# A decoder trunk's gMLP output projection: seven block products in place of eight

## The chip, the core and the metric

The kernel runs on one core of a Trainium2 chip. The metric is the time of one execution on the device in microseconds (us), from the first instruction to the last with the start and the end of the program around it. Lower is better. A run's profile is one execution taken by the hardware profiler; its span goes from the first to the last instruction.

The names in the text: TensorE (PE) multiplies matrices and writes to PSUM, which has eight buffers of 128 x 512 floats here; VectorE (DVE), ScalarE (ACT) and GpSimd (POOL) work element by element; SyncE (SP) issues most of the transfers (DMA) between the device's memory and the on-chip SBUF. Each engine works through its own queue in order.

## The reference

A trunk of two layers on 512 tokens of 1024 features. Layer 0 mixes tokens with a gMLP, then comes a gated feed-forward net with a short convolution, then a gated embedding; layer 1 has attention in place of the gMLP. The part that the change touches is the last line of the gMLP:

```python
def mixer_a(xn, w_in, g_v, w_s, b_s, w_out):
    z = jax.nn.gelu(xn @ w_in)
    u, v = jnp.split(z, 2, axis=-1)
    v = rmsnorm(v, g_v)
    ...
    s = jnp.einsum('hts,bcshd->bcthd', w, v) + b_s.T.astype(v.dtype)[None, None, :, :, None]
    s = s.reshape(B, S, A_WIDTH)
    return (u * s) @ w_out
```

Its result is added to the residual stream h, and the norm of the feed-forward net (norm_ffn) reads h next. All data are 32-bit floats.

## The kernel before, in words

Activations lie transposed, with features on the 128 partitions and the 512 tokens along the free axis: h is eight tiles h[0] to h[7] of 128 x 512. To keep float32 accuracy with TensorE's float32r, every operand x is split into a high part (a cast) and a low part (x minus the cast), and each product takes three matmuls: high by high, high by low, low by high (`mm3`, line 218; its matmul is line 229, so all stages' matmuls carry that line and are told apart by the tile they write).

Weights come in pieces of 1 MB from memory. The list of pieces, in the order in which the stages use them, is made ahead (lines 71 to 131). `load` (162) brings a piece into one of three staging buffers that take turns (tags r0 to r2, `staged`, 143). `pump` (173) cuts it into units of at most 128 x 1024 and splits each: the cast into `wh` is ACT's (line 197), the low part `wl` is DVE's (198). There are four buffers each for wh and wl, and a stage asks for units up to four ahead (`chunk`, 208), so a cast waits until matmuls have let go of an earlier unit.

A dense stage (`dense_add`, 423) runs over four chunks of 256 output features. A chunk has two units of weights; for each of its two output tiles, 8 x 3 matmuls of 512 columns add up in one PSUM buffer "d", then DVE adds it to h (431) and `Norm.take` (341) does three things with the new h tile: the split with the gain (ACT 302, DVE 303), the square (ACT 332), and the running sum of squares "acc" (POOL 337, for the last tile DVE). When all eight are in, DVE turns and reduces the sum (350, 352), TensorE adds it across partitions ("ms", 361), and the factor 1/rms goes out to memory and back to lie in rows ("line", "rstd", 376 and 401).

The feed-forward net has a second form of a stage already, the woven one (`woven_add`, 478). It takes activation tiles in pairs: tile 2p and 2p+1, each cut into a first and a second half of 256 tokens, are a 2 x 2 block matrix; the weights of 256 output features are another. Their product takes seven block products in place of eight (a scheme of Strassen's kind), over sums and differences of the blocks. `Pair` (445) makes the activations' seven operands: "edge" is the first half of tile 2p, "own" is tile 2p+1, "ones" and "twos" are differences. `begin` is called when the first tile of the pair is there, `end` when the second is. `weave` (149) makes the weights' sums on DVE (157 to 159) in a further staging buffer, "wsum", and a chunk has then three units of 1024 and one of 512. The seven products of 256 columns each add into two PSUM buffers: "dx" (a chain from which partial results "head" and "tail" are copied out by ACT) and "dy". DVE adds them to h (497, 513, 524, 525). A chunk's seventh product (number 4) is done late, inside the next chunk (`close`, 493).

The gMLP, with the names of the lines: values zv[0] to zv[3] (tiles m0 to m3) hold v; for each chunk c of 4, two tiles of u are projected (751), scaled (DVE 756), passed through GELU (ACT 758); TensorE forms "s" from zv and the masked position weights (761), DVE adds gain and bias (764) and multiplies (767), and the result is split into two tiles of the arena (770). Then `dense_add` at line 773 does the output projection. Every stage's TensorE work is issued in the order of the program as far as the data are expected in time; the compiler that orders each engine's queue may put an instruction that it expects to be ready ahead of one that it does not.

Two lines say how arena and m-tiles are used as homes for a pair's own, ones and twos:

```python
437	        if q < SLOTS:
438	            return [ap.tile([P, S], F32R, tag=f"a{x}{q}", name=f"{name}{x}") for x in "hl"]
439	        both = mp.tile([P, 2, S], F32R, tag=f"m{q - SLOTS}", name=name)
```

## Time and profile before

| what | before |
|---|---|
| median of 3 runs | 1121.63 us (1121.51 to 1121.77) |
| profiled execution | 1120.52 us |
| its span | 1118.8 us |
| mean granted TensorE clock | 0.998 |
| values and u chunks of the gMLP | to 98.5 us |
| output projection (tile d) | 100.28 to 143.81 us |
| feed-forward net's first woven stage | 242.07 to 283.25 us |

A row of a timeline has the start in us from the span's start, the time in us, the engine, the line, the operation and what it wrote from what; x2 at the end means two instructions merged, and the bracket says how long the engine had been idle and what released it. A row of the chain of work that ended last has start, time and what. A row of a tile's view has the line, engine, operation, count, and the duration in ns as least, median and greatest. Matmuls overlap, so the time of one (390 ns for 512 columns) is longer than the step from one to the next.

### The profile page before, as it was taken

To read this page: it belongs to the slowest core of one execution; us is meant where nothing else is said; L and a number is where in the kernel's file an instruction comes from. 1 tells how busy PE (TensorE), PEld (TensorE's weight loads), DVE (VectorE), ACT (ScalarE), POOL (GpSimd) and SP (SyncE) were. 2 spreads that over 40 slices of the span, in tenths; PEclk is the share of its full clock that TensorE was granted. 3 is DMA by queue.
4 is the path that set the end of the run, shared out by engine and by line. 5 is a ranking of instruction groups with operands and counts; after the bars stand their busy time and mean duration, and the time that the engine had idled before them with its cause. 6 is when DMAs were issued, how large, how long until landed. Compare 5 with 4: busy or idle time off the path is not lost.

```text
span 1118.8 us, 14875 instructions
## 1 busy us (share of the span) xinstructions
PE 1108.8 (99%) x5691; PEld 947.1 (85%) x5691; DVE 868.3 (78%) x1374; ACT 568.9 (51%) x936; POOL 103.9 (9%) x167
## 2 busy tenths in 40 slices
PE   9999999999999999999999999999999999999997
PEld 7888888889888998888888887888898889988876
DVE  5566449999788877657988997499997898785696
ACT  5733325545444544554656776255454445445543
POOL 1100210000000000022204451100000000000210
PEclk9999999999999999999999999999999999999999
DMA  8632313223331252333134224321244212522433
GB/s 296 135 114 76 113 48 113 76 76 123 142 113 39 76 189 69 101 113 113 63 88 132 76 57 151 111 93 71 76 151 136 90 38 76 189 85 88 148 103 86
DMA packets 35624, 118.40 MB, mean 106 GB/s; under 512 B 11800, under 2 KB 17440, under 8 KB 25056
## 3 DMA queue, kind: packets, MB, share of 16 engines
q1 hardware_dynamic: 34800, 116.19, 31.8%
q0 software_dynamic: 336, 0.79, 0.4%
q8 instruction: 45, 0.74, 0.3%
q10 hardware_dynamic: 416, 0.46, 0.1%
q14 instruction: 27, 0.22, 0.1%
HBM read 109.02 MB, written 2.11 MB: 99 GB/s over the span
## 4 chain that ended last, share of the span: by engine, by line
PE 68%; DVE 20%; ACT 4%; DMA 4%; issue 3%; POOL 0%; POOLq 0%; SPq 0%; ACTq 0%; DVEq 0%
PE up L229 26%; PE d L229 7%; PE dx L229 5%; DVE wl L198 5%; PE dy L229 4%; PE gate L229 4%; PE u L229 4%; PE q L229 3%; DVE c L558 3%; DVE c L559 2%; PE o L229 2%; DVE hs L551 2%; ACT wh L197 1%; PE v L241 1%; PE v L239 1%
## 5 line engine op out<-in xcount | busy, mean ns | idle before, releaser
L198 DVE TENSOR_TENSOR wl<-wraw,wh 128x1024 fp32r<-128x1024 f32 (+2 forms) x198 | 232.8, 1177 | 83.4 <-ACT wh L197 82.1
L197 ACT CAST wh<-wraw 128x1024 fp32r<-128x1024 f32 (+2 forms) x197 | 194.1, 990 | 147.9 <-PE up L229 56.1
L229 PE MATMUL up<-nf00h,wh 128*128 128x512 f32 x352 | 137.1, 390 | 0.0
L229 PE MATMUL up<-nf10h,wh 128*128 128x512 f32 x352 | 137.0, 389 | 0.0
L229 PE MATMUL up<-nf10l,wh 128*128 128x512 f32 x352 | 137.0, 389 | 0.0
L229 PE MATMUL up<-nf00l,wh 128*128 128x512 f32 x352 | 137.0, 389 | 0.0
L229 PE MATMUL up<-nf00h,wl 128*128 128x512 f32 x352 | 136.9, 389 | 0.0
L229 PE MATMUL up<-nf10h,wl 128*128 128x512 f32 x352 | 136.9, 389 | 0.0
L557 ACT ACTIVATE c<-hs,vec 128x512 f32<-128x512 f32 x88 | 71.6, 815 | 64.4 <-DVE hs L551 62.6
L558 DVE SCALAR_TENSOR_TENSOR c<-hs,vec,c 128x511 f32<-128x511 f32 x88 | 65.5, 747 | 20.4 <-ACT c L557 20.4
L229 PEld LDWEIGHTS up<-nf10h,wh 128*128 128x128 f32 x352 | 66.1, 188 | 13.7
L229 PEld LDWEIGHTS up<-nf00h,wl 128*128 128x128 f32 x352 | 66.1, 188 | 13.7
L229 PEld LDWEIGHTS up<-nf10l,wh 128*128 128x128 f32 x352 | 66.1, 188 | 13.7
L229 PEld LDWEIGHTS up<-nf00l,wh 128*128 128x128 f32 x352 | 66.1, 188 | 13.6
L229 PEld LDWEIGHTS up<-nf00h,wh 128*128 128x128 f32 x352 | 66.1, 188 | 13.6
L229 PEld LDWEIGHTS up<-nf10h,wl 128*128 128x128 f32 x352 | 66.1, 188 | 13.5
L559 DVE SCALAR_TENSOR_TENSOR c<-hs,vec,c 128x510 f32<-128x510 f32 x88 | 65.6, 748 | 2.2
L197 ACT CAST wh<-wsum 128x1024 fp32r<-128x1024 f32 x32 | 33.7, 1052 | 35.3 <-PE dy L229 11.3
L551 DVE TENSOR_TENSOR hs<-up,nf1rstd 128x512 f32<-128x512 f32 x44 | 30.1, 686 | 21.1 <-DMA nf1rstd<-nf1line 10.5
L551 DVE TENSOR_TENSOR hs<-up,nf0rstd 128x512 f32<-128x512 f32 x44 | 30.1, 686 | 20.9 <-DMA nf0rstd<-nf0line 10.4
L198 DVE TENSOR_TENSOR wl<-wsum,wh 128x1024 fp32r<-128x1024 f32 x32 | 39.1, 1221 | 9.3 <-ACT wh L197 9.2
L562 ACT ACTIVATE a<-c 128x512 f32<-128x512 f32 x44 | 27.7, 630 | 15.9 <-DVE c L559 15.8
(519 smaller groups left out, 2661.4 us busy)
## 6 DMA issues: line engine op xcount, KB each, us to landing
wraw<-in_w_up SPq DMA_DIRECT2D x44, 1024.0 KB, 4.8
wraw<-in_w_down SPq DMA_DIRECT2D x16, 1024.0 KB, 4.8
wraw<-in_w_gate SPq DMA_DIRECT2D x8, 1024.0 KB, 5.3
wraw<-in_w_down SPq DMA_DIRECT2D x8, 768.0 KB, 4.1
wraw<-in_w_u SPq DMA_DIRECT2D x4, 1024.0 KB, 10.8
wraw<-in_w_out SPq DMA_DIRECT2D x4, 1024.0 KB, 4.7
wraw<-in_w_q SPq DMA_DIRECT2D x4, 1024.0 KB, 4.8
wraw<-in_w_o SPq DMA_DIRECT2D x4, 1024.0 KB, 4.9
```

Of the source, the lines that this page charges most:

```text
L197: cast = nc.scalar.copy(hi, src)
L198: state["split"] = splits[u] = cast, nc.vector.tensor_sub(low, src, hi.bitcast(F32))
L229: nc.tensor.matmul(ps, w, x, start=first and j == 0, stop=last and j == len(todo) - 1, skip_group_check=onto)
L239: nc.tensor.matmul(ps, xh[:, s], wh[:, a:b], start=st, stop=False)
L241: nc.tensor.matmul(ps, xh[:, s], wl[:, a:b], start=False, stop=en)
L551: ins = nc.vector.tensor_mul(hs, ps, rstds[1])
L557: nc.scalar.activation(c, hs, AF.Identity, bias=v("conv_b", l * 2 * NJ + col), scale=cw[2])
L558: nc.vector.scalar_tensor_tensor(c[:, 1:], hs[:, : S - 1], cw[1], c[:, 1:], op0=ALU.mult, op1=ALU.add)
L559: nc.vector.scalar_tensor_tensor(c[:, 2:], hs[:, : S - 2], cw[0], c[:, 2:], op0=ALU.mult, op1=ALU.add)
L562: nc.scalar.activation(a, cs[0], AF.Silu)
```

## The change

The output projection of the gMLP calls `woven_add` instead of `dense_add`, and its weights are planned as woven pieces. The eight tiles u x s are made into four pairs as they come, with the arena's tiles 0 to 8 as homes for pairs 0 to 2 and m0 to m2 (the value projection's tiles) for pair 3. `Pair` is given its homes as an argument; with `soon`, which is set for pair 3, it makes the parts that the first products need first. `woven_add` learns to feed the norm, to use other buffers for head and tail (c0 and c1), and with `soon` to do product 5 ahead of product 2 in the first chunk. The feed-forward net's stages keep their behaviour. The diff, cut:

```diff
@@ -114,7 +114,7 @@
     for q, k0, k1 in FIRST:
         plan_pair(t["w_v"][2 * q : 2 * q + 2], k0, k1)
     plan_cols(t["w_u"], 4, KD)
-    plan_cols(t["w_out"], 4, KD)
+    plan_woven(t["w_out"], 4, 0, KD)
     plan_ffn(0)
     plan_cols(t["w_gate"][0], 4, KD)
     plan_cols(t["w_kv"][0:1], 1, KD)
@@ -445,26 +445,34 @@
     class Pair:
 
 
-        def __init__(self, p, edge, name):
-            self.p, self.name = p, name
+        def __init__(self, p, edge, name, homes):
+            self.homes, self.name = homes[3 * p : 3 * p + 3], name
             self.edge = edge[:, p, 0, :], edge[:, p, 1, :]
 
-        def begin(self, a):
+        def begin(self, a, soon=False):
             self.a = a
-            self.own, self.ones, self.twos = (couple(homes[3 * self.p + x], f"{self.name}_{x}") for x in range(3))
+            self.own, self.ones, self.twos = (couple(q, f"{self.name}_{x}") for x, q in enumerate(self.homes))
             hi, lo = self.edge
             nc.scalar.copy(hi, a[:, first])
             self.t = tp.tile([P, S], F32, tag="acc", name=f"{self.name}t")
             nc.vector.tensor_sub(self.t[:, first], a[:, first], a[:, second])
             nc.vector.tensor_sub(lo, a[:, first], hi.bitcast(F32))
-
-        def end(self, b):
+            if soon:
+                split(self.t[:, first], *(x[:, first] for x in self.ones))
+
+        def end(self, b, soon=False):
             t, u = self.t, tp.tile([P, S], F32, tag="sq", name=f"{self.name}u")
+            if soon:
+                split(b, *self.own)
             nc.vector.tensor_sub(t[:, second], b[:, second], self.a[:, second])
             nc.vector.scalar_tensor_tensor(u[:, first], t[:, first], -1.0, b[:, second],
                                            op0=ALU.mult, op1=ALU.subtract)
             nc.vector.scalar_tensor_tensor(u[:, second], u[:, first], -1.0, b[:, first],
                                            op0=ALU.mult, op1=ALU.subtract)
+            if soon:
+                split(u, *self.twos)
+                split(t[:, second], *(x[:, second] for x in self.ones))
+                return
             for src, (hi, lo) in ((b, self.own), (t, self.ones), (u, self.twos)):
                 split(src, hi, lo)
 
@@ -475,7 +483,7 @@
                           7: (self.ones, second), 6: (self.twos, first), 4: (self.twos, second)}[x]
             return [z[:, cols] for z in pair]
 
-    def woven_add(pairs, between):
+    def woven_add(pairs, between=None, norm=None, tags=("acc", "sq"), soon=False):
 
 
         ops = {x: [p.operand(x) for p in pairs] for x in range(1, 8)}
@@ -495,20 +503,28 @@
                 product(4, chain, w, 0, first=False)
                 nc.scalar.copy(tail[:, first], chain)
                 nc.vector.tensor_sub(h[2 * c + 1], h[2 * c + 1], tail)
+                if norm is not None:
+                    norm.take(2 * c + 1)
             return run
 
         late = None
         for c in range(4):
             top, low = h[2 * c], h[2 * c + 1]
             chain, other = psum(f"dx{c}")[:, first], psum(f"dy{c}")
-            head = tp.tile([P, S], F32, tag="acc", name=f"head{c}")
-            tail = tp.tile([P, S], F32, tag="sq", name=f"tail{c}")
+            head = tp.tile([P, S], F32, tag=tags[0], name=f"head{c}")
+            tail = tp.tile([P, S], F32, tag=tags[1], name=f"tail{c}")
             w = unit()
             product(1, chain, w, 0)
-            product(2, other[:, first], w, n)
-            nc.scalar.copy(head[:, first], chain)
-            w = unit()
-            product(5, other[:, second], w, n)
+            if c or not soon:
+                product(2, other[:, first], w, n)
+                nc.scalar.copy(head[:, first], chain)
+                w = unit()
+                product(5, other[:, second], w, n)
+            else:
+                nc.scalar.copy(head[:, first], chain)
+                w, w2 = unit(), w
+                product(5, other[:, second], w, n)
+                product(2, other[:, first], w2, n, first=False)
             product(6, chain, w, 0, first=False)
             nc.vector.tensor_sub(low[:, second], low[:, second], other[:, second])
             nc.scalar.copy(head[:, second], chain)
@@ -523,8 +539,10 @@
                     nc.scalar.copy(tail[:, second], chain)
             nc.vector.tensor_add(top, top, head)
             nc.vector.tensor_add(top, top, other)
+            if norm is not None:
+                norm.take(2 * c)
             late = close(c, chain, unit(), tail)
-            if c == 0:
+            if c == 0 and between:
                 between()
         late()
 
@@ -575,7 +593,7 @@
                 edge = at.tile([P, PAIRS, 2, N], F32R, tag="vtl", name=f"edge{i}")
                 pairs = []
                 for p in range((j1 - j0) // 2):
-                    pair = Pair(p, edge, f"act{i}_{p}")
+                    pair = Pair(p, edge, f"act{i}_{p}", homes)
                     pair.begin(up(j0 + 2 * p) if p else ahead)
                     pair.end(up(j0 + 2 * p + 1))
                     pairs.append(pair)
@@ -743,7 +761,8 @@
     for c in range(NC):
         nc.vector.tensor_scalar_mul(zv[c], zv[c], rv[:, c : c + 1])
 
-    us = []
+    edge = at.tile([P, PAIRS, 2, N], F32R, tag="vtl", name="edge")
+    us = [Pair(c, edge, f"us{c}", range(3 * PAIRS)) for c in range(PAIRS)]
     for c in range(4):
         parts = chunk(256, KD)
         ups = [psum(f"u{c}_{j}") for j in range(2)]
@@ -765,12 +784,9 @@
                 s.rearrange("p (b t) -> p b t", b=NC), sp.rearrange("p (b t) -> p b t", b=NC), v("a_norm_v", m),
                 bS[:, m : m + 1, :].to_broadcast([P, NC, P]), op0=ALU.mult, op1=ALU.add)
             nc.vector.tensor_mul(u, u, s)
-            hi = ap.tile([P, S], F32R, tag=f"ah{m}", name=f"ush{m}")
-            lo = ap.tile([P, S], F32R, tag=f"al{m}", name=f"usl{m}")
-            split(u, hi, lo)
-            us.append((hi, lo))
+            (us[c].end if j else us[c].begin)(u, soon=c == 3)
     nf = Norm("nf0", [(xp, "x", gain("norm_ffn", 0))])
-    dense_add(us, KD, nf)
+    woven_add(us, norm=nf, tags=("c0", "c1"), soon=True)
 
 
     lines = dram.tile([KD, 2, P], F32, name="lines")
```

## Prediction

> **What bounds the kernel now.** The page comes first: how full is TensorE?
>
> ```profile
> span 1118.8 us, 14875 instructions
> PE 1108.8 (99%) x5691; PEld 947.1 (85%) x5691; DVE 868.3 (78%) x1374; ACT 568.9 (51%) x936; POOL 103.9 (9%) x167
> ```
>
> TensorE (PE) is busy for all but 10 us. Time is won where it issues less work, or lost where it is made to wait. The profiled execution took 1120.52 us (1118.8 us of span and 1.72 us around it), 1.11 us less than the median of the three timed runs, 1121.63 us. I make the sum against the execution and carry its difference over to the median.
>
> Second, the chain of work that ended last, around the stage that is changed:
>
> ```profile
> 98.50 1.78 PE s L761 x16
> 100.28 43.53 PE d L229 x192
> 143.81 0.22 PE turned L781 x2
> 144.03 5.46 PE up L229 x24
> 149.49 0.13 PE nf0ms L361 x2
> ...
> 164.95 1.29 DVE hs L551 x2
> ```
>
> The output projection is the row "d": 192 matmuls of 512 columns in 43.53 us, 0.2267 us each, with no hole before, inside or behind it. The two things that follow are pinned to its end: the up projection, and the norm's small matmul nf0ms at 149.49, from which the broadcast of the norm's factor and all gating of the feed-forward net hang (VectorE's "hs" at 164.95; from there the chain runs mostly on VectorE). So what counts is by how much nf0ms moves.
>
> Third, the stretches: how much room have the other engines beside TensorE, and how much in the feed-forward net's stage that has the woven form already?
>
> ```profile
> 60.00:100.00 40.00, 40.00 (x210) 34.28 (x209) 25.20 (x33) 16.49 (x22) 0.00 (x0) 1.00 0.23 81
> 100.00:144.00 44.00, 44.00 (x198) 36.39 (x197) 22.95 (x29) 17.41 (x24) 9.33 (x6) 1.00 0.28 96
> 242.00:284.00 42.00, 41.86 (x342) 41.15 (x341) 37.21 (x50) 22.03 (x37) 0.00 (x0) 1.00 0.40 136
> ```
>
> The columns are the stretch, its length, then PE, PEld, DVE, ACT and POOL. DVE (VectorE) goes from 23 us busy in the dense stage to 37 in a woven one, and the woven ones have no work on POOL.
>
> **The change part by part.**
>
> *The products.* 4 chunks x 48 matmuls of 512 columns become 4 chunks x 7 products x 4 pairs x 3 = 336 matmuls of 256 columns. By columns that is 7/8, and would save 5.4 us. But the woven stages show what a matmul of 256 columns costs:
>
> ```profile
> 401.01 2.87 PE dy L229 x24
> ```
>
> 2.87/24 = 0.1196 us, more than half of 0.2267. So 336 x 0.1196 = 40.18 us: the saving is **3.35 us** if nothing waits. With their waits, the four woven stages took (first matmul to the next stage's first):
>
> ```profile
> 242.07 0.40 PE L229 MATMUL dx<-edge,wh 128*128 128x256 f32 x2
> 283.25 16.80 PE up L229 x74
> 370.16 0.40 PE L229 MATMUL dx<-edge,wh 128*128 128x256 f32 x2
> 411.18 54.43 PE up L229 x240
> 798.47 0.40 PE L229 MATMUL dx<-edge,wh 128*128 128x256 f32 x2
> 840.03 87.07 PE up L229 x384
> 926.94 0.40 PE L229 MATMUL dx<-edge,wh 128*128 128x256 f32 x2
> 967.95 7.05 PE up L229 x31
> ```
>
> 41.18, 41.02, 41.56 and 41.01 us, 41.19 in the mean, 1.0 us of it waiting. At that price the new stage saves 43.53 - 41.19 = **2.34 us**. I take this and add what the new stage has that those have not. The Trainium skill, "TensorE: Matmul & The Clock Gate", section "Back-to-back issue gap", gives an isolated gap of N/2.4 + 2.5 ns, 216 and 109 ns here: 41.4 against 36.7 us, an estimated saving of 4.7. The rows of both widths are of this kernel and slower, so they decide; what the rule would give is the last rival.
>
> *The start.* Before the feed-forward net's woven stages stands an extra up tile of 10.9 us, in which the last pair is prepared. Here only the 16 small matmuls "s" do, 98.50 to 100.28, and they make part of that pair's input. VectorE's timeline there:
>
> ```profile
> 98.53 0.69 DVE L756 TENSOR_TENSOR uz<-u,n0rstd 128x512 f32<-128x512 f32 x1 [0.64 <-PE u L229]
> 99.38 1.23 DVE L198 TENSOR_TENSOR wl<-wraw,wh 128x1024 fp32r<-128x1024 f32 x1 [0.16 <-ACT wh L197]
> 100.53 1.40 DVE L764 SCALAR_TENSOR_TENSOR s<-s,vec,bS 128x512 f32<-128x512 f32 x2
> 101.84 1.28 DVE L767 TENSOR_TENSOR u<-u,s 128x512 f32<-128x512 f32 x2
> 103.22 1.29 DVE L307 TENSOR_TENSOR usl<-u,ush 128x512 fp32r<-128x512 f32 x2
> ```
>
> The dense form wants u6 only after 18 matmuls, at 104.36, and has it. The woven form wants the first half of u6, split, for its tenth matmul, at 100.28 + 9 x 0.12 = 101.36 (its low part at 101.48). The weight piece ahead of s is now half as long (0.6 us less): s at 99.8, u at 101.1 to 102.3. Then the edge, by the feed-forward net's rows:
>
> ```profile
> L456 ACT CAST edge<-a x16: 406/407/411, 172.1 to 910.5; 128x256 fp32r<-128x256 f32 x16
> L459 DVE TENSOR_TENSOR edge<-a,edge x16: 414/422/427, 173.1 to 911.5; 128x256 fp32r<-128x256 f32 x16
> ```
>
> u6 at 101.7, cast to 102.1, t and then the low part by 103.0: 1.5 us late. Part of it can be filled, as nine matmuls of the next product (1.1 us) are ready; but the same VectorE queue has still five halves and two full tiles to make for the products behind (3 us, until 106.2 with what gets between), so the fourth product's twos come late too. I take **+1.3 us**. Bounds: 0, if s and u of tile 6 pass the weight piece (low part at 101.5), and 3.2, if the order stays as it is (u at 103.1, edge at 103.9, 2.4 late, and 0.8 at the twos).
>
> The new wait of m0 to m2, the value projection's tiles, is on the 16 "s" that read them, over at 100.28; ACT's cast into m1 stands behind u6 (101.7) anyway: nothing, and 0.6 us per cast behind it if the casts came first.
>
> *VectorE in the stage.* Per chunk there are three sums, four low parts, four updates of h and two of the norm:
>
> ```profile
> L198 DVE TENSOR_TENSOR wl<-wsum,wh x32: 1208/1222/1227, 235.2 to 958.2; 128x1024 fp32r<-128x1024 f32 x32
> L157 DVE TENSOR_TENSOR wsum<-wraw x16: 1212/1219/1226, 216.7 to 952.1; 128x1024 f32<-128x1024 f32 x16
> L158 DVE TENSOR_TENSOR wsum<-wsum,wraw x16: 677/684/695, 218.5 to 953.3; 128x512 f32<-128x512 f32 x16
> L513 DVE TENSOR_TENSOR h<-h,dy x16: 403/412/422, 247.6 to 960.7; 128x256 f32<-128x256 f32 x16
> L525 DVE TENSOR_TENSOR h<-h,dy x16: 676/678/689, 251.3 to 966.6; 128x512 f32<-128x512 f32 x16
> 113.22 0.74 DVE L303 SCALAR_TENSOR_TENSOR nf00l<-h,vec,nf00h 128x512 fp32r<-128x512 f32 x1
> ```
>
> 2.6 + 4.3 + 2.4 + 1.5 = 10.8 us; two such in a row overlap by 0.08 (1.28 for two of 0.68), so 9.8 of a chunk's 84 x 0.1196 = 10.05. It just fits. What the other woven stages do not have is the norm's sum on POOL, six times. In the per-layer embedding it meets a low part:
>
> ```profile
> 533.76 1.34 POOL L337 TENSOR_TENSOR n1acc<-n1acc,n1sq 128x512 f32<-128x512 f32 x1 [3.86 <-ACT n1sq L332]
> 533.86 2.32 DVE L198 TENSOR_TENSOR wl<-wraw,wh 128x1024 fp32r<-128x1024 f32 x1
> 543.82 1.72 DVE L198 TENSOR_TENSOR wl<-wraw,wh 128x1024 fp32r<-128x1024 f32 x1
> ```
>
> The low part takes 2.32 or 1.72 instead of 1.22: 0.5 to 1.1 us lost per meeting. The Trainium skill, "SBUF — State Buffer", section "Who interferes with whom", says why: a VectorE instruction with two SBUF inputs and a reading GpSimd instruction lock each other out for a whole instruction. These rows agree; and by it the dense stage, where VectorE was half idle, hid what this one cannot. With 0.5 per add, two adds a chunk, a chunk has 10.8 us, 0.75 too many, 2.3 in the three chunks that have weights behind them. Against that stands the lookahead: a chunk's first weight unit gets its buffer when the chunk before has three products left (3 x 12 x 0.12 = 4.3 us), cast (1.05) and low part (1.22) leave 2.0. I take the difference, **+0.3 us**; bounds 0 and 4.0 (1.1 per add: 12.0 a chunk, 2.0 x 3 - 2.0).
>
> *The end.* Before, nf0ms came when TensorE was free (143.81 + 5.68), the sum of squares being there 0.8 us sooner:
>
> ```profile
> 143.85 0.69 DVE L431 TENSOR_TENSOR h<-h,d 128x512 f32<-128x512 f32 x1 [0.63 <-PE d L229]
> 148.04 0.69 DVE L352 TENSOR_REDUCE nf0quarter<-nf0turn 128x16 f32<-128x512 f32 x1
> ```
>
> Woven, h7 takes a copy on ACT first, and ACT may hold it up behind a weight cast that waits for its DMA, since sums take one of the three staging buffers and loads start later. So it is in the feed-forward net (stage end 283.1):
>
> ```profile
> 282.73 1.05 ACT L197 CAST wh<-wraw 128x1024 fp32r<-128x1024 f32 x1 [1.95 <-DMA wraw<-in_w_up]
> 284.95 0.69 DVE L497 TENSOR_TENSOR h<-h,tail 128x512 f32<-128x512 f32 x1
> ```
>
> h7 then starts 1.8 us behind the end instead of 0.04; with the slack of 0.8 that is 1.0, less the 0.4 us copy of "turned" that can go first. I take **+0.6 us**; bounds 0 (TensorE is not free sooner) and 1.4.
>
> *What hides the rest.* The pairs' extra casts and differences and the first sums (on VectorE five halves of 0.42 and one tile of 0.68 more a chunk, 2.3 us with overlaps taken off, and 2.6 once) lie in the u chunks, where it is idle 15 of 40 us; uncovered they would cost up to 0.5 us at the start. No DMA is added to SP's queue; the four extra turns of the staging buffers shift later loads by one buffer, where one load now makes ACT wait 0.4 us at 561, off TensorE's path: between -0.4 and +0.4, taken as 0.
>
> **Sum:** -2.34 + 1.3 + 0.3 + 0.6 = -0.14 us, so 1120.4 for the profiled execution and **1121.5 us** for the median.
>
> **The rivals.** *The cover holds* (faster): the tile-6 work passes the weight piece, POOL's adds fall into holes and the end keeps its slack: -2.34 (1119.3 us) to -2.9 with fewer waits than its sisters, so 1119.0 us. For it: the start is ordered for it, half u6 first. Against: VectorE's row at 99.38 and its load. *VectorE becomes the bound* (slower): each POOL add costs a low part 1.1 us as at 533.86; it decides from about 0.45 us per add (10.05 + 2.0/3 = 10.7 a chunk). Then +4.0 instead of +0.3: 1125.2 us. For it: the rows at 533.86 and 543.82; against: an add that falls beside an instruction which reads PSUM meets no second SBUF input, and two of the four updates of h are such. *No waits at all, at 7/8*: the rows of 256 columns exclude it. *The rule's gap*: 4.7 instead of 3.35 with the same waits, 1120.1 us; the rows exclude it nearly.
>
> **How the numbers follow.** A measurement of this kernel can tell about 0.2%, 2.24 us, from no change. Chances: forecast 0.63 (its own range 1119.5 to 1123.8, the start's and the end's bounds), cover holds 0.13, VectorE the bound 0.23, the rule's gap 0.01. The range for 8 in 10 is 1119.2 to 1125.0: down to most of the cover case, up to the VectorE case. Faster 0.13, within 0.2% 0.64, slower 0.23.
>
> **What would show it.** In the new trace: matmuls "dx" and "dy" of the us tiles at 0.12 us; a hole of 1 to 2 us between "s" and the twelfth "dx"; low parts over 1.6 us beside "nf0acc" on POOL; nf0ms more than 5.7 us behind the last "dx". I am wrong if the stage takes under 41 us with its start (cover), or if TensorE waits in every chunk for "wl" (VectorE), or if the difference lies behind 165 us, in stages this change does not touch.

## The result and the profile after

The changed kernel takes **1133.01 us** in the median of 4 runs (1131.72 to 1134.17), the kernel before 1121.59 us (1121.51 to 1121.77, 4 runs): 1.0101 of it, 95% interval 1.0084 to 1.0119, or 11.4 us slower. The forecast was 1121.5 us and its range ended at 1125.0. The profiled execution took 1133.69 us, 13.17 us more than that of before. Where do they lie? First the head of the page after:

```profile
span 1131.9 us, 15285 instructions
PE 1113.0 (98%) x5835; PEld 956.3 (84%) x5835; DVE 902.0 (80%) x1427; ACT 584.4 (52%) x969; POOL 104.8 (9%) x167
```

TensorE has the 144 matmuls more that were planned (336 for 192), and is idle for 18.9 us of its span (1131.9 - 1113.0) instead of 10.0. The waits of TensorE by what ended them (engine, line, total us, times, the longest) name most of the new idle time:

```profile
PE up L229 <- ACT wh L197: 3.3, 1, 3.3
PE nf0ms L361 <- DVE nf0quarter L352: 1.4, 1, 1.4
PE dx L229 <- ACT head L520: 1.4, 2, 1.1
PE up L229 <- ACT nf00h L302: 1.2, 1, 1.2
...
PE o L229 <- DVE wl L198: 1.0, 1, 1.0
PE up L229 <- DVE nf00l L303: 0.6, 1, 0.6
PE dx L229 <- DVE edge L459: 0.5, 1, 0.5
PE dx L229 <- ACT head L524: 0.3, 1, 0.3
```

Only the rows "dx" (2.2 us) lie in the changed stage; those with nf0 stand at its end, and the rows 3.3 and 1.0 are in layer 1's attention, at 701 us. A comparison of the two traces at fixed points, from the first instruction that each stage issues on TensorE (its last one, for the two rows that say so), shows the steps:

| point | before | after | later by |
|---|---|---|---|
| output projection, first matmul | 100.03 | 100.33 | 0.30 |
| its end ("turned") | 143.65 | 144.60 | 0.95 |
| nf0ms | 149.33 | 154.16 | 4.83 |
| VectorE's first hs | 164.95 | 169.91 | 4.96 |
| feed-forward net over ("pin") | 465.45 | 473.11 | 7.66 |
| attention's output projection, first "o" | 640.61 | 648.26 | 7.65 |
| its last "o" | 700.05 | 714.42 | 14.37 |
| last gate tile "gt" | 1111.12 | 1124.18 | 13.06 |

The 0.30 at the start is within what single profiles differ by (the first matmul lies between 99.80 and 100.64 in all of them). So there are four losses: 0.65 us in the stage, 3.9 between its end and nf0ms, 2.7 between hs and pin, 6.7 in the attention 500 us later. Behind the attention 1.3 us come back.

**The stage.** The window of after that the prediction showed of before (stretch, length, PE, PEld, DVE, ACT, POOL, the granted clock, DMA):

```profile
100.00:144.00 44.00, 41.84 (x338) 40.57 (x336) 43.00 (x57) 25.80 (x45) 7.34 (x4) 1.00 0.31 112
```

VectorE is busy 43.0 of 44 us, where the dense stage had 22.95 and the sister stage 37.21 of 42. The stage took 44.27 us (100.33 to 144.60) for 40.18 us of products; the dense one, measured the same way, took 43.62 (100.03 to 143.65). TensorE's timeline shows where it waits, at the start and twice later:

```profile
102.53 0.38 PE L229 MATMUL dx<-edge,wh 128*128 128x256 f32 x1
103.36 0.38 PE L229 MATMUL dx<-edge,wh 128*128 128x256 f32 x1 [0.45 <-DVE edge L459]
103.58 0.27 PE L229 MATMUL dx<-edge,wl 128*128 128x256 f32 x1
103.70 0.39 PE L229 MATMUL dy<-us,wh 128*128 128x256 f32 x1
104.41 0.39 PE L229 MATMUL dx<-us_2h,wh 128*128 128x256 f32 x1 [0.32 <-ACT head L524]
...
126.56 0.39 PE L229 MATMUL dx<-us_2h,wh 128*128 128x256 f32 x1 [1.10 <-ACT head L520]
137.15 0.39 PE L229 MATMUL dx<-us_2h,wh 128*128 128x256 f32 x1 [0.28 <-ACT head L520]
```

A bracket counts from the modelled end of the matmul before; by starts, the steps 102.53 to 103.36 and 103.70 to 104.41 cost 1.3 us more than 0.12 each. At 126.56 the copy of "head" came late on ScalarE. ScalarE's timeline says why:

```profile
125.10 0.63 ACT L332 ACTIVATE nf0sq<-h 128x512 f32<-128x512 f32 x1 [1.02 <-POOL nf0acc L337]
...
126.15 0.36 ACT L520 COPY head<-dx 128x256 f32<-128x256 f32 x1
```

The square waited for POOL to let go of the square before it, and a cast (125.64) and the copy that TensorE needed stood behind it.

**The tail.** POOL's and VectorE's timelines at the end of the stage, POOL's first:

```profile
135.06 4.02 POOL L337 TENSOR_TENSOR nf0acc<-nf0acc,nf0sq 128x512 f32<-128x512 f32 x2 [7.64 <-ACT nf0sq L332]
145.46 3.01 POOL L337 TENSOR_TENSOR nf0acc<-nf0acc,nf0sq 128x512 f32<-128x512 f32 x2 [6.38 <-ACT nf0sq L332]
```
```profile
135.61 2.32 DVE L198 TENSOR_TENSOR wl<-wsum,wh 128x1024 fp32r<-128x1024 f32 x1
137.85 1.78 DVE L303 SCALAR_TENSOR_TENSOR nf00l<-h,vec,nf00h 128x512 fp32r<-128x512 f32 x1
...
145.96 1.35 DVE L303 SCALAR_TENSOR_TENSOR nf00l<-h,vec,nf00h 128x512 fp32r<-128x512 f32 x1
147.43 2.12 DVE L198 TENSOR_TENSOR wl<-wraw,wh 128x1024 fp32r<-128x1024 f32 x1
149.47 0.68 DVE L505 TENSOR_TENSOR h<-h,tail 128x512 f32<-128x512 f32 x1
150.08 1.21 DVE L198 TENSOR_TENSOR wl<-wraw,wh 128x1024 fp32r<-128x1024 f32 x1
...
153.33 0.69 DVE L352 TENSOR_REDUCE nf0quarter<-nf0turn 128x16 f32<-128x512 f32 x1
```

Where POOL adds, a low part takes 2.32 or 2.12 us in place of 1.22, a split 1.78 or 1.35 in place of 0.74. From 147.43 on each instruction starts where the one before ends, until the split of h7 is over: VectorE has a queue, not gaps. h7 (line 505) starts 4.9 us behind the stage's end, where 1.8 was forecast, and TensorE stands still for tile h7's split and for nf0quarter.

**The clock.** One window of before, then two of after; the column behind POOL's is the granted clock:

```profile
155.00:160.00 5.00, 5.00 (x23) 4.13 (x22) 0.00 (x0) 1.05 (x1) 0.00 (x0) 1.00 0.03 3
```
```profile
150.00:155.00 5.00, 2.06 (x6) 1.35 (x7) 4.15 (x8) 1.25 (x2) 0.00 (x0) 0.85 0.56 180
155.00:160.00 5.00, 5.00 (x13) 3.84 (x13) 0.45 (x3) 0.34 (x1) 2.41 (x2) 0.50 0.11 30
```

Behind a stretch in which TensorE was busy for 2.06 of 5 us, the clock is at one half: 13 matmuls in place of 23 in the five us after it. PE counts as fully busy there; only the clock column and the count show it.

**The attention.** SyncE's timeline of before, and then of after (the issue of loads; a row stands for several when x is over 1):

```profile
651.85 21.77 SPq L167 DMA_DIRECT2D wraw<-in_w_o  x2
```
```profile
659.26 0.33 SPq L167 DMA_DIRECT2D wraw<-in_w_o  x1
680.64 5.71 SPq L167 DMA_DIRECT2D wraw<-in_w_up  x2
686.58 0.34 SPq L167 DMA_DIRECT2D wraw<-in_w_o  x1
```

The last piece of w_o leaves at 686.58, behind two pieces that are used after it. That is when the last "pv" matmul ends (685.83 + 0.72): the piece has got the staging buffer r1, which the attention uses for its weights, "pts4". TensorE's timeline of after shows the price:

```profile
701.18 0.50 PE L229 MATMUL up<-nf10h,wh 128*128 128x512 f32 x1 [3.31 <-ACT wh L197]
702.92 0.70 PE L229 MATMUL o<-oh,wl 128*128 128x512 f32 x1 [1.01 <-DVE wl L198]
```

The two waits are 4.3 us, and the mean clock of 0.96 in the 40 us around them (680 to 720) stands for 1.6 more; together that is most of the 6.7 us.

### The profile page after: what moved, and what is told of

The parts are those of the page before. It is cut to its first block, busy times and chain, and to the rows that moved or that the text cites. A ratio compares the mean times of both kernels' runs of the same rounds, so it can differ in the third digit from the quotient of the medians.

```text
span 1131.9 us, 15285 instructions
## 1 busy us (share of the span) xinstructions
PE 1113.0 (98%) x5835; PEld 956.3 (84%) x5835; DVE 902.0 (80%) x1427; ACT 584.4 (52%) x969; POOL 104.8 (9%) x167
## 4 chain that ended last, share of the span: by engine, by line
PE 79%; DVE 5%; issue 2%; ACT 1%; POOLq 0%; POOL 0%; DVEq 0%; ACTq 0%
PE up L229 42%; PE dx L229 6%; PE dy L229 5%; PE d L229 5%; PE q L229 4%; PE gate L229 4%; PE o L229 3%; DVE wl L198 2%; PE pv L1065 1%; PE pin L229 1%; PE k L229 1%; PE gt L239 1%; PE gt L240 1%; PE gt L241 1%; ACT wh L197 1%
## 5 line engine op out<-in xcount | busy, mean ns | idle before, releaser
L229 PEld LDWEIGHTS up<-nf00h,wh 128*128 128x128 f32 x352 | 66.8, 190 | 15.5 <-ACT nf00h L302 1.6
L229 PEld LDWEIGHTS up<-nf10l,wh 128*128 128x128 f32 x352 | 66.1, 188 | 13.5
L197 ACT CAST wh<-wsum 128x1024 fp32r<-128x1024 f32 x40 | 42.1, 1052 | 43.2 <-PE dy L229 12.9
L198 DVE TENSOR_TENSOR wl<-wsum,wh 128x1024 fp32r<-128x1024 f32 x40 | 50.0, 1251 | 13.3 <-ACT wh L197 13.3
```

Of the source, the lines that this page charges most:

```text
L197: cast = nc.scalar.copy(hi, src)
L198: state["split"] = splits[u] = cast, nc.vector.tensor_sub(low, src, hi.bitcast(F32))
L229: nc.tensor.matmul(ps, w, x, start=first and j == 0, stop=last and j == len(todo) - 1, skip_group_check=onto)
```

## The experiments

The theory: the loss is the staging order (6.7 us) and POOL's sum of squares, which holds up a full VectorE (the rest, half of it through the clock). Each kernel was profiled and timed against the kernel before on the same chip, and times of different chips are compared by ratio only. The ratios are those on record; plain medians differ from them by up to 0.0006.

**1. The staging order: a_turn and b_turn.** The four sums take four turns of the staging buffers, and four is one more than a full round of three. a_turn takes two turns more after the attention, which completes the round; b_turn gives the kernel before one turn too many.

```diff
     state["tags"] = [0, 1, 2]
+    state["turn"] += 2      # a_turn, on the changed kernel
+    state["turn"] += 1      # b_turn, on the kernel before
```

> The changed kernel with two more turns of the staging buffers after the attention, so that the last piece of w_o falls into the same buffer as before. Theory 'staging': the four sums in the new woven stage turned the buffers on by four, so this piece now lies behind the last use of pts4, and about 6.7 us of the loss (the matmuls of o end 14.4 us later than before where they began 7.7 later) arise there. Expected: o ends about 7.7 us later than before, and the time falls by 6 to 7 us to about 1126.5 us. Rival 'late chain': the loss at o comes from the earlier stages being out of step, not from the buffer; then o still ends 14 us later and the time stays at about 1133.

> The kernel before, with nothing changed but one more turn of the staging buffers after the attention: the last piece of w_o falls into the buffer of pts4, as in the changed kernel. Theory 'staging': 6 to 7 us slower than before, about 1128 us, all of it between the last pv and the end of o. Rival 'late chain': no change, 1121.6 us.

Measured: a_turn 1126.3 us, 1.0043 of the kernel before (1.0026 to 1.0060), 6.7 us less than the change; b_turn 1128.04 us, 1.0057 (1.0042 to 1.0072), 6.4 more than the kernel before on that chip (1121.6). b_turn's trace has the same waits, the second of 1.00 us behind this one:

```profile
695.11 0.50 PE L229 MATMUL up<-nf10h,wh 128*128 128x512 f32 x1 [3.32 <-ACT wh L197]
```

The theory holds from both sides: about 6.5 of the 11.4 us have nothing to do with the output projection. All further versions of the change have a_turn's line.

**2. POOL's sums or the order of ScalarE: a_dve and a_tail.** a_dve gives the running sum to VectorE; a_tail leaves it on POOL and lets the last tail's copy pass the weight cast ahead of it on ScalarE.

```diff
-            self.square(k, nc.vector if k == KD - 1 else None)
+            self.square(k, nc.vector if k == KD - 1 or self.name == "nf0" else None)   # a_dve
...
-            late = close(c, chain, unit(), tail)
+            late = close(c, chain, take() if c == 3 and norm is not None else unit(), tail)   # a_tail
```

> a_turn, and in the new stage the norm's running sum is added by VectorE for all tiles instead of by POOL for six of seven. Theory 'lock': VectorE's instructions beside POOL's adds were stretched by some 5 us in all (2.32 and 2.12 instead of 1.22, 1.78 and 1.35 instead of 0.75); without POOL they keep their usual length, six adds of 0.6 us = 3.6 come on VectorE, and ACT's square that waited 1.0 us for POOL does not hold up the head copy; expected stage end about 1 us and nf0ms 1 to 3 us earlier, time 1 to 5 us less than a_turn. Rival 'queue order': what counts is where the casts and the tail stand; more work on VectorE makes nf0ms later, 0 to 3 us slower than a_turn.

> a_turn, and the weight unit of the second up piece is no longer asked for before the last product of the last chunk but after it, so that ACT's cast for it stands behind the copy of tail. Theory 'queue order': the copy waited 2.6 us behind that cast (done 147.3, stage end 144.6) and VectorE's low part of the same unit another 2.1; expected nf0ms 2 to 4 us earlier than in the changed kernel (154.2), less idle time of TensorE, the granted clock back near 1.0 from 155 to 160, and 3 to 6 us less than a_turn. Rival 'VectorE load': VectorE has a backlog anyway and the copy's place changes nothing; nf0ms stays within 0.7 us of 154.

Measured: a_dve 1121.53 us, 1.0002 (0.9993 to 1.0011); a_tail 1126.26, 1.0041 (1.0027 to 1.0056), as a_turn: the gain of 3 to 6 us expected of it did not come, and its rival did. In a_tail the tail's copy came 1.0 us sooner (146.34) and h7's subtraction at once behind it, but that one now met POOL, and a low part slipped in before the sum's turning, as VectorE's timeline shows:

```profile
147.21 1.77 DVE L505 TENSOR_TENSOR h<-h,tail 128x512 f32<-128x512 f32 x1
...
151.31 1.21 DVE L198 TENSOR_TENSOR wl<-wraw,wh 128x1024 fp32r<-128x1024 f32 x1
152.44 0.70 DVE L350 STREAM_TRANSPOSE nf0turn<-nf0acc 128x512 f32<-128x512 f32 x1
```

nf0ms stayed at 154.0. In a_dve, by contrast, VectorE has six adds more (6 x 0.68 us) and is done sooner: the stage took 42.3 us (100.29 to 142.62) without a wait in its middle, nf0ms came at 151.45, and the clock stayed up. VectorE's timeline of a_dve, with a low part at its usual length, and the window behind:

```profile
147.36 1.21 DVE L198 TENSOR_TENSOR wl<-wraw,wh 128x1024 fp32r<-128x1024 f32 x1
```
```profile
155.00:160.00 5.00, 5.00 (x24) 4.14 (x23) 1.22 (x1) 1.61 (x2) 0.29 (x1) 1.00 0.05 4
```

This is what the Trainium skill, "SBUF — State Buffer", "Who interferes with whom", states: with two SBUF inputs VectorE shares a read port with GpSimd, and one waits for the other's whole instruction. The rows agree: 0.6 to 1.1 us per meeting, and none without POOL's adds.

**3. Is it the meeting or the work of the adds: a_noadd and dense_dve.** a_noadd leaves out the squares of the first six tiles, and with them all of POOL's adds; one add, of the last two tiles, stays on VectorE. Its factor is then not the model's, so that only its times are of use. dense_dve makes a_dve's edit in the kernel before.

```diff
-            if self.acc is None:
+            if self.acc is None or self.name == "nf0" and k < KD - 1:   # a_noadd
```

> The changed kernel with the staging mended, and the first norm's running sum over its first six tiles left out: the squares of the last two tiles alone are added. Theory (what hurts is POOL's adds beside VectorE's low parts, and not the adds' own work): 0 to 2 us less than the version with the sum on VectorE, so 1119.5 to 1121.5 us. Rival (VectorE's whole load in this stage is what is late, its sums with it): clearly less, under 1119.5 us, with the norm's matmul at 148 us or sooner.

> The kernel before with the running sum of the first norm's squares on VectorE instead of POOL, and nothing else. Theory (the POOL adds cost time only where VectorE has no slack; in the kernel before it has slack in this stage): as before, within 0.5 us. Rival (the adds on POOL cost time in the kernel before, too, so that the change's products would still be slower than a kernel before so mended): 1 to 3 us less than before.

Measured: a_noadd 1123.74 us and dense_dve 1123.87 on a chip where the kernel before took 1124.08, 2.5 us more than on the one that the expectation's numbers come from; by ratio 0.9997 (0.9988 to 1.0006) and 0.9996 (0.9987 to 1.0005). So the adds on VectorE cost nothing that can be told from none at all (a_dve 1.0002), on POOL they cost 4.8 us (a_turn against a_dve), and in the dense stage, with VectorE half idle, it made no difference where they were. The theory held both times.

The adds are not the whole of the end, though. From the start of the stage's last matmul to nf0ms it is 5.9 us in the kernel before, 9.7 in the change, 9.0 in a_dve and still 8.2 in a_noadd, where nothing is left on POOL to meet.

**4. The clock: warm.** Eight matmuls into an unused PSUM buffer ahead of nf0ms, on a_turn:

```diff
+                if l == 0 and j == 0 and not s:
+                    warm = psum("warm")
+                    for i in range(8):
+                        nc.tensor.matmul(warm, ones, xs[0][0], start=True, stop=True)
```

> a_turn (sum on POOL, staging as before) with eight matmuls of 512 columns into an unused buffer placed where TensorE waits ahead of nf0ms. They add no result and fill about 1.8 us of its 4 us of idle time there. Theory 'clock': the idle time itself lowers the granted clock (0.50 from 155 to 160 in the changed kernel, and 1.5 to 2.8 us lost between nf0ms and the embedding's projection); with the gap filled the clock stays at 1.0 and the time falls by 1 to 2 us below a_turn although nothing is computed sooner. Rival: the loss behind nf0ms is the gating's chain coming late, not the clock; then no gain.

Measured: 1124.01 us, 1.0015 (1.0006 to 1.0025), against a_turn's 1.0043 (1.0026 to 1.0060). nf0ms came no sooner (154.40), but the stretch behind it ran at full clock; the window of warm, and under it that of a_turn:

```profile
155.00:160.00 5.00, 5.00 (x23) 4.10 (x22) 1.72 (x4) 1.06 (x1) 2.41 (x2) 1.00 0.19 61
```
```profile
155.00:160.00 5.00, 5.00 (x18) 4.03 (x17) 0.46 (x3) 1.05 (x1) 2.41 (x2) 0.73 0.14 28
```

From hs to pin warm lost 0.07 us against the kernel before, a_turn 1.5, after 2.7. By ratio, useless matmuls made the kernel faster. Their exact worth stays loose: the two kernels ran on different chips, and the two intervals all but touch.

**5. Why does a shorter stage bring nothing: nosoon, v1, v3, v4.** a_dve's stage is 1.3 us shorter than the dense one (42.33 for 43.62, first matmul to turned), and its time is the same. nosoon undoes the early order of the last pair; v1, v3 and v4 thin out, step by step, what VectorE and ScalarE do between the stage's end and the norm's factor (the loads, casts and low parts of the next weights come later).

```diff
-            (us[c].end if j else us[c].begin)(u, soon=c == 3)
+            (us[c].end if j else us[c].begin)(u, soon=False)
...
-    woven_add(us, norm=nf, tags=("c0", "c1"), soon=True)
+    woven_add(us, norm=nf, tags=("c0", "c1"))
```

That is nosoon. v1, in `woven_add`'s last chunk and in the first up tile:

```diff
-            w = unit()
+            lean = c == 3 and norm is not None
+            w = take() if lean else unit()
             if late:
                 late()
+            if lean:
+                pump(state["next"] + 3)
...
-            parts = chunk(256, KD)
+            lean = l == 0 and j == 0
+            parts = chunk(256, KD, ahead=2 if lean else WBUFS)
...
+                    if lean and not s:
+                        pump(state["next"] + 2)
```

v3 puts h7's square ahead of its split, asks for one weight unit less at the start and puts a low part there behind the last product u x s, and puts two low parts behind the norm's sum; v4 moves these two, with their casts:

```diff
+                        behind(splits[u][1], norm.last)
+                        behind(splits[u + 1][1], norm.last)
```
```diff
-                        behind(splits[u][1], norm.last)
-                        behind(splits[u + 1][1], norm.last)
+                        after = nc.vector.tensor_copy(const.tile([P, 1], F32, name="after"), norm.root[:, :1])
+                        for x in (u, u + 1):
+                            behind(splits[x][0], norm.squared)
+                            behind(splits[x][1], after)
```

> a_dve without the early order: pair 3 is made like the others and the first chunk does product 2 before product 5. It undoes one part of the change. If the start is set by VectorE's queue (my prediction's step), the edge comes no later (it stands first in the queue in both), but own is wanted before ones, and the twos later: stage 0.3 to 1.5 us longer than in a_dve. If the order buys nothing, within 0.2 us.

> a_dve (running sum of the norm on VectorE, staging as before), and in the last chunk and behind it the up projection's weight units are asked for two at a time later: the second one after product 4 of chunk 2, the third and fourth after the norm's begin. Theory 'queue order at the tail': with VectorE's load eased, the weight pieces that stand ahead of h5, h7 and the reduction in its queue are what is left; nf0ms moves from 8.8 us behind the stage's end to 6 to 7.5, time 1 to 2.5 us less than a_dve (about 1119.5). Rival 'backlog': VectorE has as much to do as before, only in another order, and the up projection then waits for its weights; nf0ms moves by less than 0.7 and the time stays within 0.7 us of a_dve.

> v1, and in addition: the last square of the norm goes ahead of the last split, the third and fourth weight units' low parts stand behind the norm's reduction in VectorE's queue, and in the first chunk the half weight unit's low part stands behind the last product u x s. Theory: the start's wait (1.1 us: 0.45 for the edge, 0.32 and parts) shrinks to 0.3 to 0.6, and nf0ms comes 5.7 to 6.5 us behind the stage's end; 1 to 2 us less than v1, about 1118.3. Rival 'backlog': what is put off at the start is missing in the first chunk and the stage's end does not move; then no more than 0.5 us less than v1.

> v3 with two more moves at the end of the stage: ScalarE's casts of the third and fourth units stand behind its last square, and VectorE's low parts of these units behind the root of the norm's factor, so that VectorE is idle while POOL works out the root. Theory (with staging and the POOL adds mended, what is left over the kernel before is the way from the last tail to the norm's factor, where VectorE's low parts and POOL's root disturb each other): the norm's matmul ends near 148.2 us, the factor stands near 164 us as in the kernel before, and the time is near 1120.5 us, about 1.1 us less than before. Rival (the loads of the next stage or the factor's transfers set the end of this path, whatever VectorE does): no gain, 1121.6 plus or minus 0.7 us.

Measured: nosoon 1122.56 us, 1.0000 (0.9991 to 1.0010); v1 1122.4, 1.0002 (0.9993 to 1.0012); v3 1122.79, 1.0010 (1.0000 to 1.0019); v4 1122.52, 0.9990 (0.9981 to 0.9999). The kernel before took 1121.86 us on the chip of the first three and 1124.08 on v4's. The early order that nosoon undoes is worth about 0.3 us of the stage and nothing in the time; v1 and v3 missed what was expected of them. v3 had its last matmul of the stage at 142.28 and nf0ms back at 149.27, as early as in the kernel before, and was not faster.

What they did change is the end: from the stage's last matmul to nf0ms it is 8.5 us in v1, 7.0 in v3 and 5.9 in v4, the 5.9 of the kernel before. So what made the end longer was mostly the order, casts and low parts of the next weights standing ahead of h7 and the norm's sum (and the last square behind the last split), and for the smaller part POOL's adds (9.7 against 9.0 and 8.2). The chain of v3, and then of v4, behind nf0ms:

```profile
150.93 2.68 POOL nf0rt L418
...
153.90 9.02 DMA nf0line<-nf0rt
...
163.21 4.61 DMA nf0rstd<-nf0line
```
```profile
149.62 1.65 POOL nf0rt L419
...
151.55 9.95 DMA nf0line<-nf0rt
...
161.79 5.50 DMA nf0rstd<-nf0line
...
167.31 1.29 DVE hs L586 x2
```

In the kernel before the same steps took 1.66, 8.62 and 3.65 (its chain at 150.42, 152.36 and 161.28). v3's root met VectorE's low part (2.68); v4 took that away, as expected, but hs came at 167.31 and not near 164. The loads that wait for the buffers of the held-back low parts now go beside the factor's two transfers (SyncE's timeline of v4; in the kernel before the first of them leaves at 146.02):

```profile
153.75 26.09 SPq L167 DMA_DIRECT2D wraw<-in_w_up  x3
```

The DMA share from 155 to 160 us is 0.81 in v4, 0.96 in v3 and 0.03 in the kernel before. What was won ahead of nf0ms was lost ahead of hs. That the loads slow the two transfers is likely for v4 (15.5 us together, 12.3 in the kernel before), and not shown: v3's took 13.6, and dense_dve's 13.5 with a DMA share of 0.04.

**6. Does hs set the end: b_root.** The kernel before, with POOL's root worked out three times.

```diff
-        nc.gpsimd.tensor_tensor(r, m, minus_half[:, :n], op=ALU.pow)
+        [nc.gpsimd.tensor_tensor(r, m, minus_half[:, :n], op=ALU.pow) for i in range(3 if name == "nf0" else 1)]
```

> The kernel before, with POOL's root of the first norm's factor worked out three times over in place of once (the same values written again): 3.3 us more between nf0ms and the factor, on POOL alone, which has nothing else to do then. Theory (after the output projection the way nf0ms, root, line, rstd, hs sets the end, and TensorE's matmuls do not): hs comes 3.3 us later, the gMLP's following stages end 3 to 4 us later, and the time is 3 to 4 us more, 1.0030 plus or minus 0.001. Rival (TensorE's work in the stages behind sets the end, with some slack for the factor): under 1 us more, 1.0000 to 1.0010.

Measured: 1128.1 us, 1.0044 (1.0031 to 1.0057), against 1123.47 on its chip, somewhat more than the 3 to 4 us expected. POOL's row, and VectorE's first hs:

```profile
150.64 5.67 POOL L414 TENSOR_TENSOR nf0rt<-nf0m,minus_half 128x8 f32<-128x8 f32 x3 [8.60 <-DVE nf0m L412]
```
```profile
170.17 1.29 DVE L551 TENSOR_TENSOR hs<-up,nf0rstd 128x512 f32<-128x512 f32 x2 [15.35 <-DMA nf0rstd<-nf0line]
```

The root took 4.0 us more, hs came 5.2 later (the transfers were 1.0 slower in this run, and 0.2 was there already), and pin with it. The profiled versions, a line each, against the kernel before's nf0ms at 149.33, first matmul of the feed-forward net's woven stage at 242.07, hs at 164.95 and pin at 465.45:

| kernel | nf0ms later by | woven stage later by | hs later by | pin later by | clock, 155 to 160 |
|---|---|---|---|---|---|
| a_dve | 2.12 | 2.21 | 1.58 | 2.03 | 1.00 |
| dense_dve | 0.57 | 0.58 | 1.86 | 1.94 | 1.00 |
| nosoon | 2.41 | 2.47 | 2.08 | 2.31 | 1.00 |
| v4 | -0.89 | 0.88 | 2.36 | 2.36 | 1.00 |
| a_noadd | 1.56 | 3.23 | 2.53 | 3.08 | 1.00 (0.66 from 150) |
| v1 | 2.64 | 2.72 | 2.59 | 2.60 | 1.00 |
| v3 | -0.06 | 0.04 | 2.89 | 3.50 | 1.00 |
| b_root | 0.22 | 5.33 | 5.22 | 5.22 | 1.00 |
| warm | 5.07 | 5.20 | 5.41 | 5.48 | 1.00 |
| a_turn | 4.76 | 6.40 | 4.71 | 6.22 | 0.73 |
| a_tail | 4.68 | 7.67 | 5.00 | 7.49 | 0.50 |
| after | 4.83 | 7.84 | 4.96 | 7.66 | 0.50 |

Two roads lead to pin, and the later one counts. One is TensorE's own: nf0ms, then 408 matmuls "up". In a_dve, nosoon, v1 and a_noadd TensorE has no wait on it, so its woven stage and pin come as much later as nf0ms, plus the clock's part in a_noadd; a_turn, a_tail and after are the same with more of the clock. The other road goes over hs: in v3, v4, dense_dve and b_root nf0ms moved by less than 1 us, and TensorE waits for VectorE behind the late hs. The first road in a_dve's chain, and the second in TensorE's timelines of v3 and then of b_root:

```profile
151.81 92.64 PE up L229 x408
```
```profile
250.15 0.58 PE L229 MATMUL dy<-act_0h,wh 128*128 128x256 f32 x1 [2.16 <-DVE h L534]
```
```profile
172.65 0.50 PE L229 MATMUL up<-nf00h,wl 128*128 128x512 f32 x1 [3.18 <-DVE wl L198]
```

The 300 us of matmuls up to pin give next to nothing back. A profile is one execution: dense_dve's medians equal the kernel before's although its profiled hs is 1.9 us later, mostly by its transfers, so a difference of 1 or 2 us in this table is not yet one between kernels.

## Why the prediction was wrong, step by step

- **The products** (3.35 us by 0.1196 each): right. The steps between matmuls that did not wait are 0.12 us (103.58 to 103.70), and the rule's shorter gap is out.
- **The start, +1.3**: right in size, 1.3 us by starts, and the first wait is the one that was looked for (edge). The second was to come from the twos on VectorE; TensorE waited for the copy "head" on ScalarE instead, so that part of the agreement is luck. Without the early order of the last pair (nosoon) the stage takes 0.3 us more.
- **VectorE and POOL, +0.3 with a bound of 4.0 and the rival at 1125.2**: the mechanism was right, and was even priced (1.1 us per add), but 0.3 came from taking 0.5 per add and subtracting a lookahead of 2.0. The rows show 0.6 to 1.1. In the stage itself this made the two waits at 126.56 and 137.15, 1.38 us, on copies by ScalarE and not on low parts; with the adds on VectorE the stage is 1.9 us shorter (42.33 for 44.27). Without them the sum of products, sisters' waits and start is met: 41.19 + 1.3 = 42.5 for 42.33. The rest of the queue came out at the end, where the prediction didn't look for it: it counted the stage and the end as two separate sums, though the end starts with what the stage leaves in VectorE's queue.
- **The end, +0.6, bounds 0 and 1.4**: this step failed. Measured 3.9 us. The late copy on ScalarE was there as forecast (1.0 us by a_tail), but removing it alone brought nothing. 0.7 us go with POOL's adds moved to VectorE and 1.5 with the six squares left out; over 2 us are VectorE's low parts of the next weights (147.43 and 150.08) with ScalarE's casts for them, ahead of h7 and of the sum, and v4, which holds them back, has the kernel before's 5.9 us again. The prediction counted a copy held up on ScalarE and no queue on VectorE.
- **What follows nf0ms**: "what counts is by how much nf0ms moves" was right as to the place (hs, then pin), and missed the clock: behind waits of 1.2, 0.6 and 1.4 us within 4.4 us it was at one half for over 5 us, worth another 2.7 in the profile.
- **The staging buffers, between -0.4 and +0.4, taken as 0**: the largest failure, 6.7 us in the profile and 6.5 by a_turn and b_turn. The prediction had counted the four turns and their shift by one buffer. It priced the shift by the one wait that the trace before showed (561 us), and did not ask what else lives in a buffer with that name: r1 holds the attention's "pts4" until its last product.
- **The rivals**: "VectorE becomes the bound" came true in part: VectorE was full and the adds cost it what that rival said, but TensorE never waited in the stage for a weight's low part (wl), and most of the loss arose at the end and through the clock. The attention's loss no rival had. Staging mended, the change stands at 1.0043, or 1126.3 us, 1.1 above that rival's 1125.2; so near a hit by another path is luck.
- **A slip in its sums**: the start's and the end's bounds give 1119.6 to 1124.2 for the forecast's own range, not 1119.5 to 1123.8. Nothing hangs on it.
- The last condition for being wrong, a difference behind 165 us "in stages this change does not touch", is the one that was met.

Mended in both points, the change gives the time of the kernel before, and v4 at best 0.1% less (0.9990, 0.9981 to 0.9999). With the adds on VectorE it takes 1.3 us out of the stage, and what follows takes it back: in a_dve the way from the stage's last matmul to nf0ms is 3.1 us longer, 2.4 of it TensorE standing still, and in v4, where that is gone, hs comes late through POOL and two transfers. Which of the two roads holds the timed runs, whose difference is 0.1% or less, one profile of each can't tell.

What stays open: how much of the clock's 2.7 us the timed runs hold, and whether v4's gain would grow if the next weights were loaded before the factor's transfers rather than beside them; that version was not made.

## What to carry to other kernels

When an edit takes one more turn of a rotating buffer, follow the rotation to the end of the program: count the turns modulo the number of buffers, and look for every other user of each buffer's name. When a stage fills an engine up, the next stage inherits its queue; price the end of the stage with that queue in it, and take shared-port work (POOL's adds, here) off the full engine's path first. And before counting on a shorter stage, find what waits behind it: here the norm's small matmul, at which TensorE stood still for what it had saved, and a factor that goes through memory, which moved pin one for one when it alone was delayed (b_root).

## What the runs showed of the hardware that was not expected

The granted clock fell to 0.50 over the 5 us after three waits whose longest was 1.43 us, TensorE having been busy 2.06 of 5 us. The Trainium skill, "TensorE: Matmul & The Clock Gate", "Why this matters for your kernels", says to leave no gap of over about 3 us between bursts of matmuls; here no wait was that long. Their sum (1.17 + 0.55 + 1.43 = 3.15 us in 4.4 us) doesn't settle it either: a_noadd had a clock of 0.50 after waits of 0.5 and 1.4 us, while it stayed at 1.00 in a_dve with 0.4, 0.5 and 1.4, in v1 with 0.3 and 2.4, and in warm with its eight filler matmuls. What decides stays open. By windows of 1 us, the time at one half adds up to 3.4 us in a_turn and a_noadd and to 6.8, twice that, in after and a_tail (after: 0.75 from 153 to 154, 0.50 from there to 160, 0.83 to 161; a_turn: 0.63, 0.50, 0.50 and 0.66 from 154 to 158). Up to there after and a_turn are the same program, so the clock's price changes from one execution to another.

A transfer of 2 KB from POOL (nf0line) took 8.6 us in the kernel before, with the DMA otherwise idle, 9.2 in dense_dve, idle too, and 9.95 in v4, beside a load; the one of 256 KB behind it took 3.65, 4.3 and 5.50.
